# Interleaving two tensors: eight tiles with separate output buffers, or six longer tiles woven in place

## The chip, the cores and the metric

The kernel runs on one core of a Trainium2 chip. The metric is the device time of one execution in microseconds. Three timed runs of the kernel before gave a median of 314.32 us, from 314.16 to 314.33.

A core has five engines that run their own instruction streams, and this kernel uses three of them. VectorE copies data inside the on-chip memory (SBUF, 128 partitions). SyncE (SP) and ScalarE (ACT) only issue transfers here: SP the loads, ACT the stores. The transfers themselves run on 16 DMA engines, which both issuing engines share. SP's transfers form one queue and ACT's another. Engines wait for each other, and for transfers, through semaphores; a transfer adds 16 to its semaphore when all of it has landed.

## The reference

`x` and `y` are float32 of shape 32 x 256 x 1024, 33.55 MB each. The output alternates their elements along the last axis:

```python
result = np.zeros((batch, seq, dim * 2), dtype=np.float32)
result[..., 0::2] = x
result[..., 1::2] = y
```

No arithmetic is done. 67.11 MB have to be read and 67.11 MB written. Since the interleaving runs along the last axis, the three tensors can be treated as flat: output elements 2i and 2i + 1 are x[i] and y[i].

## The kernel before

The flat inputs are cut into n = 8 tiles of 128 x 8192 elements. In a tile each partition holds W = 8192 consecutive elements of x and of y, 32 KiB each, and the 64 KiB of output that belong to them. H = 4096 is half of W.

There are two buffers for x (`xt`), two for y (`yt`) and two for the output (`ot`), each of 32 KiB per partition. Tile k uses `xt[k % 2]` and `yt[k % 2]`. Its output is made in two halves, h = 0 and h = 1, and half h always uses `ot[h]`.

- **Loads (SP, lines 42 to 53).** Tile 0's x comes in two DMAs of 16 KiB rows, every later x and every y in one DMA of 32 KiB rows (4 MiB). The first two tiles' loads are issued without a wait. From tile 2 on, x of tile k waits until VectorE has made the third copy of tile k - 2, and y until the fourth, by the counter `woven`.
- **Copies (VectorE, lines 55 to 70).** For each half: one copy of 4096 columns of x into the even columns of `ot[h]` (L67), one of 4096 columns of y into the odd ones (L70). From tile 1 on, the x copy waits until the store of the half before in the same buffer has landed (`osem[h]`). That makes 32 copies.
- **Stores (ACT, lines 72 to 86).** Each half is stored in one DMA of 32 KiB rows as soon as its two copies are done. The very first is cut in two, 8 KiB and 24 KiB of each row, with a semaphore of its own for the first part.
- **End (lines 88 to 94).** ACT waits for the last store from `ot[0]` and clears semaphores; SP waits for the last store from `ot[1]`.

The order on each engine is the order of the code. There is no planner. One extra step in `tile_interleave_kernel` moves the first two DMAs of SP ahead of the barrier that opens the program, so that they are issued at 0.00 and 0.42 us; the next load is issued at 1.90 us.

Of the kernel before, what the change touches and what calls it, by code (L numbers as in the profile page):

```python
# [3 lines left out]


def _interleave(nc, x, y, out):
    P = 128
    W = 8192
    H = W // 2  # L10

    total = 1
    for s in x.shape:
        total *= s
    n = total // (P * W)
    assert n * P * W == total

    def rows(ap, names, k):
        flat = ap.rearrange("b s d -> (b s d)")
        return flat[k * names : (k + 1) * names].rearrange("(p w) -> p w", p=P)  # L20

    fp32 = mybir.dt.float32
    xt = [nc.alloc_sbuf_tensor(f"xt{b}", [P, W], fp32).ap() for b in (0, 1)]
    yt = [nc.alloc_sbuf_tensor(f"yt{b}", [P, W], fp32).ap() for b in (0, 1)]
    ot = [nc.alloc_sbuf_tensor(f"ot{b}", [P, W], fp32).ap() for b in (0, 1)]

    xsem = [nc.alloc_semaphore(f"xsem{b}") for b in (0, 1)]
    hsem = nc.alloc_semaphore("hsem")
    qsem = nc.alloc_semaphore("qsem")
    ysem = [nc.alloc_semaphore(f"ysem{b}") for b in (0, 1)]  # L30
    woven = nc.alloc_semaphore("woven")
    osem = [nc.alloc_semaphore(f"osem{b}") for b in (0, 1)]


    cuts = [0, W // 4, W]
    parts = [slice(a, b) for a, b in zip(cuts, cuts[1:])]

    xs = [rows(x, P * W, k) for k in range(n)]
    ys = [rows(y, P * W, k) for k in range(n)]
    os_ = [rows(out, 2 * P * W, k) for k in range(n)]  # L40

    nc.sync.dma_start(out=xt[0][:, :H], in_=xs[0][:, :H]).then_inc(xsem[0], 16)
    nc.sync.dma_start(out=xt[0][:, H:], in_=xs[0][:, H:]).then_inc(hsem, 16)

    for k in range(n):
        b = k % 2
        if k >= 2:
            nc.sync.wait_ge(woven, 4 * (k - 2) + 3)
        if k:
            nc.sync.dma_start(out=xt[b], in_=xs[k]).then_inc(xsem[b], 16)  # L50
        if k >= 2:
            nc.sync.wait_ge(woven, 4 * (k - 2) + 4)
        nc.sync.dma_start(out=yt[b], in_=ys[k]).then_inc(ysem[b], 16)

    for k in range(n):
        b = k % 2
        for h in (0, 1):
            c = slice(h * H, (h + 1) * H)
            if h == 0:
                nc.vector.wait_ge(xsem[b], 16 * (k // 2 + 1))  # L60
            elif k == 0:
                nc.vector.wait_ge(hsem, 16)
            if k:
                nc.vector.wait_ge(osem[h], 16 * k)
            if (k, h) == (1, 0):
                nc.vector.wait_ge(qsem, 16)
            nc.vector.tensor_copy(out=ot[h][:, 0::2], in_=xt[b][:, c]).then_inc(woven, 1)  # L67
            if h == 0:
                nc.vector.wait_ge(ysem[b], 16 * (k // 2 + 1))
            nc.vector.tensor_copy(out=ot[h][:, 1::2], in_=yt[b][:, c]).then_inc(woven, 1)  # L70

    for k in range(n):
        for h in (0, 1):
            nc.scalar.wait_ge(woven, 4 * k + 2 * h + 2)
            if (k, h) == (0, 0):
                for c in parts[:-1]:
                    nc.scalar.dma_start(
                        out=os_[k][:, c], in_=ot[h][:, c]
                    ).then_inc(qsem, 16)
                c = parts[-1]  # L80
                nc.scalar.dma_start(out=os_[k][:, c], in_=ot[h][:, c]).then_inc(osem[h], 16)
                continue
            nc.scalar.dma_start(
                out=os_[k][:, h * W : (h + 1) * W], in_=ot[h]
            ).then_inc(osem[h], 16)

    nc.scalar.wait_ge(osem[0], 16 * n)
    used = sorted(s.num for s in [*xsem, hsem, qsem, *ysem, woven, osem[0]])
    assert used == list(range(used[0], used[-1] + 1)), used
    nc.scalar.sem_clear(range(used[0], used[-1] + 1))  # L90
    nc.sync.nop(nofuse=True).wait_op(osem[1], 16 * n, "sem-ge").then_inc(
        osem[1], -16 * n
    )


def kernel(tc, x, y, out):
    nc = tc.nc
    tc.close()
    tc.compile()

    _interleave(nc, x, y, out)

    blocks = nc.main_func.blocks
    for engine in (mybir.EngineType.SP, mybir.EngineType.SP):
        opening = blocks[0].instructions
        at, moved = next(
            (b, i)
            for b in blocks[1:]
            for i in b.instructions
            if i.engine == engine and i.opcode == "DMACopy"  # L110
        )
        assert not (moved.sync_info and moved.sync_info.on_wait)
        body = at.instructions
        body.remove(moved)
        gate = next(
            n
            for n, i in enumerate(opening)
            if i.engine == engine and i.opcode == "Drain"
        )
        opening.insert(gate, moved)  # L120
        at.instructions = body
        blocks[0].instructions = opening


# [1 line left out]
_INS = ['x', 'y']  # L126
_OUTS = [((32, 256, 2048), 'float32')]


# [23 lines left out]
```

## Time and profile before

| What | us |
|---|---|
| median of three runs | 314.32 |
| span of the profiled execution, first to last instruction | 312.9 |
| what lies around the span (median less span) | 1.4 |
| VectorE busy, 32 copies | 72.0 |
| VectorE waiting at L67 for stores to land | 206.5 |
| one copy of 128 x 4096, L67 and L70 | 2.295 and 2.288 |
| a 4 MiB store, issue to landing (median) | 34.1 |
| a 4 MiB load of y, issue to landing (median) | 41.5 |

The profiled execution's own time is its span and what lies around it; its page lists the span alone. A page shows, for 40 equal slices of the span, the busy tenths of an engine and of the 16 DMA engines together. The time from issue to landing of a transfer holds the time that it stood behind others in its queue. q1 in the profile is SP's queue, the loads; q10 is ACT's, the stores.

### The profile page before, as it was taken

The page shows a single profiled execution, that of the slowest core. Times are in us where ns is not written, and L with a number is a line of the kernel's source. Part 1 is how long each engine was busy: PE and PEld are TensorE (multiplying, and loading weights), DVE is VectorE, ACT ScalarE, POOL GpSimd, SP SyncE. Part 2 cuts the span into 40 slices and gives each one's busy share as a digit, 9 for nine tenths or more (in the row PEclk, how much of TensorE's full clock was granted, in tenths as well). Part 3 has the DMA queues.
Part 4 walks back from the last instruction along what each step waited for, and adds up shares of the span by engine and source line. Part 5 has one row for each costly group of instructions (what it writes and reads, how often), then busy time and mean ns, then how long its engine had stood idle before and what let it go on. Part 6 is the DMA issues. An engine that isn't in the chain of part 4 may idle for free.

```text
span 312.9 us, 114 instructions
## 1 busy us (share of the span) xinstructions
DVE 72.0 (23%) x32; POOL 0.2 (0%) x4
## 2 busy tenths in 40 slices
DVE  0216000501305023050220503205032050415410
POOL 0000000000000000000000000000000000000000
DMA  8999999999999999999999999999999999999998
GB/s 337 467 402 436 436 402 419 452 457 415 427 444 411 461 402 469 402 469 402 469 402 465 406 440 432 423 448 402 469 402 469 402 469 402 469 402 448 423 423 381
DMA packets 4896, 134.22 MB, mean 429 GB/s; under 512 B 544, under 2 KB 544, under 8 KB 544
## 3 DMA queue, kind: packets, MB, share of 16 engines
q1 hardware_dynamic: 2448, 67.11, 50.1%
q10 hardware_dynamic: 2448, 67.11, 49.7%
HBM read 67.11 MB, written 67.11 MB: 429 GB/s over the span
## 4 chain that ended last, share of the span: by engine, by line
DMA 82%; DVE 12%; issue 0%
DMA out_dram<-ot 76%; DMA yt<-in_y_dram 6%; DVE ot L70 6%; DVE ot L67 6%
## 5 line engine op out<-in xcount | busy, mean ns | idle before, releaser
L67 DVE COPY ot<-xt 128x4096 f32<-128x4096 f32 x16 | 36.7, 2295 | 213.8 <-DMA out_dram<-ot 206.5
L70 DVE COPY ot<-yt 128x4096 f32<-128x4096 f32 x16 | 36.6, 2288 | 12.3 <-DMA yt<-in_y_dram 12.3
L137 POOL MEMSET const-bfloat16-1.0<- 128x1 bf16 x1 | 0.1, 103 | 0.0
L137 POOL MEMSET const-uint8-127<- 128x1 uint8 x1 | 0.1, 102 | 0.0
L137 POOL MEMSET const-float32-0.0<- 128x1 f32 x1 | 0.1, 100 | 0.2 <-issue 0.2
L137 POOL MEMSET const-float32-1.0<- 128x1 f32 x1 | 0.1, 99 | 0.0
## 6 DMA issues: line engine op xcount, KB each, us to landing
out_dram<-ot ACTq DMA_DIRECT2D x15, 4096.0 KB, 34.1
yt<-in_y_dram SPq DMA_DIRECT2D x8, 4096.0 KB, 41.5
xt<-in_x_dram SPq DMA_DIRECT2D x7, 4096.0 KB, 24.3
xt<-in_x_dram SPq DMA_DIRECT2D x2, 2048.0 KB, 9.5
out_dram<-ot ACTq DMA_DIRECT2D x1, 3072.0 KB, 32.8
out_dram<-ot ACTq DMA_DIRECT2D x1, 1024.0 KB, 16.3
```

The lines of the kernel that those rows point to most:

```text
L67: nc.vector.tensor_copy(out=ot[h][:, 0::2], in_=xt[b][:, c]).then_inc(woven, 1)
L70: nc.vector.tensor_copy(out=ot[h][:, 1::2], in_=yt[b][:, c]).then_inc(woven, 1)
L137: nc = _bacc.Bacc("TRN2", target_bir_lowering=False, num_devices=1)
```

## The change

The tiles become six: five of 11008 columns and one of 10496, so that rows of a load are 43 KiB (41 KiB in the last tile). There are no separate output buffers. Instead there are two regions `R[0]` and `R[1]` of 86 KiB per partition. Tile k of N columns uses `R[k % 2]`: x is loaded into its first N columns, y into the next N, and the 2N output elements are made in the same place. The first half of the region then holds the output of the first N/2 pairs ("low"), the second half that of the others ("high"). Two smaller buffers help: `park` of N/2 columns, and `last` of 2752.

With h = N/2, VectorE makes these copies for a tile, in this order:

1. the upper half of x into `park`;
2. the lower half of x spread to the even columns of low, from the top down: first the columns h/2 to h (they go to columns h to 2h, where the parked half of x was), then the columns 0 to h/2 by way of `last`, since their targets overlap them: three copies;
3. after y has landed, the lower half of y to the odd columns of low. Low is complete, and ACT stores it;
4. the upper half of y to the odd columns of high, the first h/2 directly and the other h/2 by way of `last`: three copies;
5. `park` to the even columns of high. High is complete, and ACT stores it.

That is nine copies per tile, three of h columns and six of h/2: 54 in all. Each copy but the first carries a wait, in the instruction itself, for the copy before it to be complete (`step`). With the separate waits for x (six, and one for the first part of tile 0) and for y (six) the code issues 67 VectorE instructions; the short description of the change counts 81, and the code does not say what the other 14 are.

A load of x of tile k >= 2 waits until low of tile k - 2 has been stored, and a load of y until high of tile k - 2 has been stored. x of tile 0 comes in two DMAs, 16 KiB and 27 KiB of each row; VectorE waits for both. The first store, low of tile 0, is issued in two parts, 8 KiB and 35 KiB of each row, with one semaphore for both. There are 13 loads and 13 stores, where there were 17 and 17.

```diff
@@ -4,92 +4,128 @@
 from concourse import mybir
 
 
+TILES = [11008] * 5 + [10496]
+FIRST = 4096
+EARLY = 2048
+
+
 def _interleave(nc, x, y, out):
     P = 128
-    W = 8192
-    H = W // 2
+    n = len(TILES)
+    N_MAX = max(TILES)
 
     total = 1
     for s in x.shape:
         total *= s
-    n = total // (P * W)
-    assert n * P * W == total
+    assert sum(TILES) * P == total
+    assert all(N % 2 == 0 for N in TILES)
 
-    def rows(ap, names, k):
+    starts = [sum(TILES[:k]) for k in range(n)]
+
+    def rows(ap, words, k):
         flat = ap.rearrange("b s d -> (b s d)")
-        return flat[k * names : (k + 1) * names].rearrange("(p w) -> p w", p=P)
+        a = starts[k] * P * words
+        return flat[a : a + TILES[k] * P * words].rearrange("(p w) -> p w", p=P)
 
     fp32 = mybir.dt.float32
-    xt = [nc.alloc_sbuf_tensor(f"xt{b}", [P, W], fp32).ap() for b in (0, 1)]
-    yt = [nc.alloc_sbuf_tensor(f"yt{b}", [P, W], fp32).ap() for b in (0, 1)]
-    ot = [nc.alloc_sbuf_tensor(f"ot{b}", [P, W], fp32).ap() for b in (0, 1)]
+    R = [nc.alloc_sbuf_tensor(f"R{b}", [P, 2 * N_MAX], fp32).ap() for b in (0, 1)]
+    park = nc.alloc_sbuf_tensor("park", [P, N_MAX // 2], fp32).ap()
+    SPARE = 2752
+    last = nc.alloc_sbuf_tensor("last", [P, SPARE], fp32).ap()
 
     xsem = [nc.alloc_semaphore(f"xsem{b}") for b in (0, 1)]
-    hsem = nc.alloc_semaphore("hsem")
-    qsem = nc.alloc_semaphore("qsem")
+    fsem = nc.alloc_semaphore("fsem")
     ysem = [nc.alloc_semaphore(f"ysem{b}") for b in (0, 1)]
-    woven = nc.alloc_semaphore("woven")
-    osem = [nc.alloc_semaphore(f"osem{b}") for b in (0, 1)]
+    step = nc.alloc_semaphore("step")
+    lsem = [nc.alloc_semaphore(f"lsem{b}") for b in (0, 1)]
+    hsem = [nc.alloc_semaphore(f"hsem{b}") for b in (0, 1)]
+
+    xs = [rows(x, 1, k) for k in range(n)]
+    ys = [rows(y, 1, k) for k in range(n)]
+    os_ = [rows(out, 2, k) for k in range(n)]
 
 
-    cuts = [0, W // 4, W]
-    parts = [slice(a, b) for a, b in zip(cuts, cuts[1:])]
+    count = 0
 
-    xs = [rows(x, P * W, k) for k in range(n)]
-    ys = [rows(y, P * W, k) for k in range(n)]
-    os_ = [rows(out, 2 * P * W, k) for k in range(n)]
+    def copy(to, of):
+        nonlocal count
+        made = nc.vector.tensor_copy(out=to, in_=of)
+        if count:
+            made = made.wait_op(step, count, "sem-ge")
+        made.then_inc(step, 1)
+        count += 1
 
-    nc.sync.dma_start(out=xt[0][:, :H], in_=xs[0][:, :H]).then_inc(xsem[0], 16)
-    nc.sync.dma_start(out=xt[0][:, H:], in_=xs[0][:, H:]).then_inc(hsem, 16)
+    def halvings(m):
+        while m > SPARE:
+            assert m % 2 == 0
+            yield m // 2, m
+            m //= 2
+        yield 0, m
 
-    for k in range(n):
+    done = []
+    for k, N in enumerate(TILES):
+        b = k % 2
+        h = N // 2
+        X = R[b][:, :N]
+        Y = R[b][:, N : 2 * N]
+        low = R[b][:, :N]
+        high = R[b][:, N : 2 * N]
+
+        if k == 0:
+            nc.vector.wait_ge(fsem, 16)
+        nc.vector.wait_ge(xsem[b], 16 * (k // 2 + 1))
+        copy(park[:, :h], X[:, h:])
+        for i, j in halvings(h):
+            if i:
+                copy(low[:, 2 * i : 2 * j : 2], X[:, i:j])
+            else:
+                copy(last[:, :j], X[:, :j])
+                copy(low[:, 0 : 2 * j : 2], last[:, :j])
+        nc.vector.wait_ge(ysem[b], 16 * (k // 2 + 1))
+        copy(low[:, 1::2], Y[:, :h])
+        done.append([count])
+        for i, j in halvings(h):
+            i, j = h - j, h - i
+            if j < h:
+                copy(high[:, 2 * i + 1 : 2 * j : 2], Y[:, h + i : h + j])
+            else:
+                copy(last[:, : j - i], Y[:, h + i : h + j])
+                copy(high[:, 2 * i + 1 : 2 * j : 2], last[:, : j - i])
+        copy(high[:, 0::2], park[:, :h])
+        done[-1].append(count)
+
+    nc.sync.dma_start(out=R[0][:, :FIRST], in_=xs[0][:, :FIRST]).then_inc(fsem, 16)
+    nc.sync.dma_start(
+        out=R[0][:, FIRST : TILES[0]], in_=xs[0][:, FIRST:]
+    ).then_inc(xsem[0], 16)
+    for k, N in enumerate(TILES):
         b = k % 2
         if k >= 2:
-            nc.sync.wait_ge(woven, 4 * (k - 2) + 3)
+            nc.sync.wait_ge(lsem[b], 16 * (k // 2) + (16 if b == 0 else 0))
         if k:
-            nc.sync.dma_start(out=xt[b], in_=xs[k]).then_inc(xsem[b], 16)
+            nc.sync.dma_start(out=R[b][:, :N], in_=xs[k]).then_inc(xsem[b], 16)
         if k >= 2:
-            nc.sync.wait_ge(woven, 4 * (k - 2) + 4)
-        nc.sync.dma_start(out=yt[b], in_=ys[k]).then_inc(ysem[b], 16)
+            nc.sync.wait_ge(hsem[b], 16 * (k // 2))
+        nc.sync.dma_start(out=R[b][:, N : 2 * N], in_=ys[k]).then_inc(ysem[b], 16)
 
-    for k in range(n):
+    for k, N in enumerate(TILES):
         b = k % 2
-        for h in (0, 1):
-            c = slice(h * H, (h + 1) * H)
-            if h == 0:
-                nc.vector.wait_ge(xsem[b], 16 * (k // 2 + 1))
-            elif k == 0:
-                nc.vector.wait_ge(hsem, 16)
-            if k:
-                nc.vector.wait_ge(osem[h], 16 * k)
-            if (k, h) == (1, 0):
-                nc.vector.wait_ge(qsem, 16)
-            nc.vector.tensor_copy(out=ot[h][:, 0::2], in_=xt[b][:, c]).then_inc(woven, 1)
-            if h == 0:
-                nc.vector.wait_ge(ysem[b], 16 * (k // 2 + 1))
-            nc.vector.tensor_copy(out=ot[h][:, 1::2], in_=yt[b][:, c]).then_inc(woven, 1)
+        for c, sem, ready in zip((0, N), (lsem[b], hsem[b]), done[k]):
+            nc.scalar.wait_ge(step, ready)
+            cuts = [c, c + N]
+            if (k, c) == (0, 0):
+                cuts = [0, EARLY, N]
+            for i, j in zip(cuts, cuts[1:]):
+                nc.scalar.dma_start(out=os_[k][:, i:j], in_=R[b][:, i:j]).then_inc(sem, 16)
 
-    for k in range(n):
-        for h in (0, 1):
-            nc.scalar.wait_ge(woven, 4 * k + 2 * h + 2)
-            if (k, h) == (0, 0):
-                for c in parts[:-1]:
-                    nc.scalar.dma_start(
-                        out=os_[k][:, c], in_=ot[h][:, c]
-                    ).then_inc(qsem, 16)
-                c = parts[-1]
-                nc.scalar.dma_start(out=os_[k][:, c], in_=ot[h][:, c]).then_inc(osem[h], 16)
-                continue
-            nc.scalar.dma_start(
-                out=os_[k][:, h * W : (h + 1) * W], in_=ot[h]
-            ).then_inc(osem[h], 16)
-
-    nc.scalar.wait_ge(osem[0], 16 * n)
-    used = sorted(s.num for s in [*xsem, hsem, qsem, *ysem, woven, osem[0]])
+    assert n % 2 == 0
+    nc.scalar.wait_ge(hsem[0], 16 * (n // 2))
+    nc.scalar.wait_ge(lsem[1], 16 * (n // 2))
+    used = sorted(s.num for s in [*xsem, fsem, *ysem, step, *lsem, hsem[0]])
     assert used == list(range(used[0], used[-1] + 1)), used
     nc.scalar.sem_clear(range(used[0], used[-1] + 1))
-    nc.sync.nop(nofuse=True).wait_op(osem[1], 16 * n, "sem-ge").then_inc(
-        osem[1], -16 * n
+    nc.sync.nop(nofuse=True).wait_op(hsem[1], 16 * (n // 2), "sem-ge").then_inc(
+        hsem[1], -16 * (n // 2)
     )
```

## The prediction

> **What bounds the kernel now.** I read the page from the top: which engine is busy, then the DMA rows, then the chain that ended last, then rates by stretch, then DMA issues.
>
> ```profile
> span 312.9 us, 114 instructions
> ...
> DVE 72.0 (23%) x32; POOL 0.2 (0%) x4
> ...
> DMA  8999999999999999999999999999999999999998
> ...
> q1 hardware_dynamic: 2448, 67.11, 50.1%
> q10 hardware_dynamic: 2448, 67.11, 49.7%
> HBM read 67.11 MB, written 67.11 MB: 429 GB/s over the span
> ```
>
> VectorE works 23% of the span. The 16 DMA engines are 9 or more tenths busy in every slice but the first and last, and the load queue (q1) and the store queue (q10) together fill 99.8%. The bytes, 134.22 MB, are fixed by the problem. So the transfers bound the kernel, and an edit counts only if it changes what the DMA engines spend per byte or leaves both queues empty at once. VectorE's 206.5 us of waiting for stores costs nothing in itself. The chain confirms it; columns are start, length, what:
>
> ```profile
> 76.83 2.29 DVE ot L67
> 79.12 2.21 DVE ot L70
> ...
> 81.36 34.17 DMA out_dram<-ot
> 115.53 0.02 issue
> 115.55 2.29 DVE ot L67
> ```
>
> A period is 115.55 - 76.83 = 38.72 us, and it moves four DMAs of 4 MiB (two loads, two stores): 9.68 us each. In the trace's packet records a row is one packet, and rows of 8, 16, 24 and 32 KiB take 309, 611, 912 and 1213 ns: 301.3 ns per 8 KiB and some 8 ns fixed, with 9 ns for the packet that signals completion. Each engine carries 8 rows of a DMA.
>
> Rates by stretch (start:end, length, DVE, POOL, clock, DMA share, GB/s) show where the engines are not at that pace:
>
> ```profile
> 0.00:7.00 7.00, 0.00 (x0) 0.20 (x4) 1.00 0.88 337
> ...
> 27.00:32.00 5.00, 1.61 (x1) 0.00 (x0) 1.00 0.96 375
> ...
> 115.00:270.00 155.00, 35.97 (x16) 0.00 (x0) 1.00 1.01 434
> ```
>
> Against 434 GB/s the start loses 7 x (1 - 337/434) = 1.6 us, and 27 to 32 us, when the first store begins beside the loads, 5 x (1 - 375/434) = 0.7 us. Nothing else is lost before the last slice.
>
> ```profile
> xt<-in_x_dram SPq DMA_DIRECT2D x2, 2048.0 KB, 9.5
> ...
> out_dram<-ot ACTq DMA_DIRECT2D x1, 1024.0 KB, 16.3
> ```
>
> The 1 MiB store is 8 rows of 8 KiB per engine, 2.5 us alone; it took 16.3. Issued at 24.24, its first packet came at 28.64 (4.4 us, 3.6 load rows), and then each small row waited for one 32 KiB load row: 8 x (0.31 + 1.21) = 12.2. So the queues take turns row by row.
>
> **The change, part by part.** Sums are against this execution: 312.9 us of span and 314.32 - 312.9 = 1.4 us to the median around it, which I leave as it is (three runs within 314.16 to 314.33).
>
> *Fewer, longer rows.* Loads go from 17 DMAs to 13, stores from 17 to 13: 34 to 26, and data packets per engine from 272 to 208. Overhead per DMA, low end: 9.68 - 32 x 0.3013 = 0.04 us, from the period. High end: 8 x 0.008 + 0.009 = 0.07, from the packet records. Saving 8 x 0.04 = 0.3 to 8 x 0.07 = 0.6. I take 0.3, since the period is a whole elapsed time and packets may overlap a little. Rows over 32 KiB are not in this trace; that they run as one packet at the same pace is an extrapolation (a rival below).
>
> *VectorE.* The code issues 54 copies: per tile three of 5504 columns and six of 2752 (5248 and 2624 in the last). Today's 4096 columns take 2.29. A 5504 copy in proportion is 3.08; a 2752 copy lies between 1.54 (in proportion) and 2.29 (no smaller than the full one). A tile is 18.5 to 23.0 us. The wait in each copy ends the overlap of 0.08 between neighbours (2.29 long, 2.21 apart) and adds some 0.03 of wake-up (copy ends 24.20, ACT's store begins 24.24): 0.1 each, 1 per tile. That is 117 to 145 us in all against 313, hidden by DMA as long as a queue has work. Behind a waiting copy stand only later copies; the store that waits is ACT's, and through the store SP's next load. Two places can lose the cover.
>
> *The first round.* All 23 MB of the first two tiles' loads are issued without a wait. Half a tile is 11008/8192 x 9.68 = 13.0 us of DMA. y0 lands at 21.91 + 2 x 3.33 = 28.6 (today's landing plus the longer halves); after one 3.08 copy ACT issues at 31.7; the first packet follows 4.4 us (as today) to 5.9 us (3.6 rows of 1.63) later: 37. Loads run meanwhile; x1 has 4 left, y1 13. The 8 KiB part takes turns with 43 KiB rows: 8 x (0.31 + 1.63) = 15.5, to 52.5, and y1 has 4 left. The 35 KiB rest (8 rows of 1.33) shares with that until about 60, then runs alone to 67.3. SP's x2 waits for it: the load queue is empty from 60 to 67.7 plus 4.4 to 5.9, about 73. Behind x2 on SP stands y2, which waits for high0 anyway. The engines are not idle, since high0 (ready 31.7 + 3 x 1.54 + 3.08 + waits = 40) follows at once. Cost of this dry load queue: 0 if sharing is as smooth as later, 0.7 at most if the queue's restart costs what the first store did at 27 to 32. Both slow stretches in the trace are first uses of a queue, which a restart is not, so I take 0. The first store's own 0.7 stays.
>
> *Steady state.* From 73 on the load queue switches half a DMA after the store queue (high0 has 7 of 13 left), so each load is issued some 13 us before its turn, and low_k, ready 3.5 us after y_k lands, also has some 9 to spare. Nothing is added.
>
> *The tail.* At 73 the loads have done four halves (52), the stores 13.0 + 5.8: a lead of 33. Equal turns keep it, less 1.2 for the last tile's shorter load rows: 32 at the loads' end. Low5 and high5 are 2 x 12.4 of that, so high4 has 7.2 left. Low5 needs 0.4 for landing, one copy (2.94), and up to 1 us to its first packet (0.99 at the start): 4.4. Margin 2.8 us. High5 needs another 8 to 10 on VectorE, under 12.4 of low5. So nothing is exposed, but this is the thinnest cover.
>
> *Start and end.* Two x0 loads of 16 and 27 KiB rows go out first, instead of two of 16; y0 is issued at about 1.9 as now, with 13 us of loads ahead of it. The final waits stand on two stores as now. 0.
>
> [...]
>
> **Sum:** 314.32 - 0.3 = 314.0.
>
> **The rivals.**
> 1. *Tail gap (slower).* At the end VectorE weaves the first half of the last tile with no store left, so both queues are empty. It decides once high4 has under 4.4 us left when y5 lands, which is when x2's first packet comes after 76 instead of 73. The most it can cost is 4.4 plus the small effects: 315 to 318.4, middle 316. For it: a margin of 2.8 at the end of a long count, and landing, copy and issue in a row before low5. Against: all rows used are from this trace, and the turns were equal in steady state. 0.17.
> 2. *Rows over 32 KiB cut in two (the change doesn't do what it says).* 23 of the 26 DMAs have such rows, 8 more packets each: 184 x 5 to 8 ns = 0.9 to 1.5, less 0.3: 315.1 or a little under. No row in the trace exceeds 32 KiB. With it I count a dry queue's restart at 0.7 and longer rows slowing the first store. 0.10, of which 0.09 beyond +0.2%.
> 3. *A larger gain.* Overhead at the high end (0.6), and the 0.7 loss at 27 to 32 smaller: 313.0 to 313.7. For: the packet records' fixed 8 ns. Against: the first store starts in the same manner. 0.21.
> 4. *Forecast:* transfers stay saturated, 313.7 to 314.9, likeliest 314.0. 0.52.
>
> **Numbers.** 0.2% (0.63 us) is about what a measurement of this kernel can tell from no change. Faster: rival 3, 0.21. Same: 0.52 + 0.01 = 0.53. Slower: 0.17 + 0.09 = 0.26. The range 313.4 to 316.5 leaves out about 0.08 below (rival 3's low part) and 0.08 above (rival 1's upper part). The forecast's own range is 313.7 to 314.9.
>
> **What would show it.** Right: 3328 data packets and 416 completions (q1 and q10 at 1872 each), both queues near 50%, a period of 52.0 us per tile, VectorE at 117 to 145 us, high4 still storing when the last y lands. Rival 1: a slice below 9 tenths near 285 us and a chain with DVE between the last loads and low5. Rival 2: packets well above 1872 per queue. A rate under 434 GB/s where both queues are full would make the whole sum wrong.

## The result and the profile after

The changed kernel took 315.71 us in the median of five runs (314.70 to 316.88), beside 314.27 for the kernel before: a ratio of 1.0046, interval 1.0028 to 1.0064. Run again beside its variants it took 314.87 (11 runs, 314.62 to 315.91) where the kernel before took 314.20: 1.0023, interval 1.0014 to 1.0031. So it is slower, by 0.7 to 1.4 us. Its single times scatter over 2.2 us in the first group and 1.3 in the second; those of the kernel before beside them lie within 0.2 (five runs) and 0.7 (35 runs). The forecast was 0.3 us faster. The profiled execution is the slowest of the five, 316.88 us, of which 315.6 is span; the second profile is of 314.78 us, span 313.5.

The page of the changed kernel, first execution:

```profile
span 315.6 us, 134 instructions
...
DVE 111.1 (35%) x54; POOL 0.2 (0%) x4
...
DMA  9999999999999999999999999999999999999994
...
q1 hardware_dynamic: 1872, 67.11, 49.7%
q10 hardware_dynamic: 1872, 67.11, 49.2%
q14 instruction: 1, 0.01, 0.0%
```

Much is as forecast: 1872 packets in each queue, so a 43 KiB row is one packet, and VectorE's work runs beside the transfers. At 111 us it is under the 117 to 145 forecast. Two things are new. The DMA engines are only 4 tenths busy in the last slice, where they were 8 before. And there is a third queue, q14, with one packet of instructions, which the page of before does not have.

Rates by stretch (start:end, length, DVE, POOL, clock, DMA share, GB/s), in the same execution:

```profile
0.00:7.00 7.00, 0.00 (x0) 0.20 (x4) 1.00 0.95 363
27.00:32.00 5.00, 3.34 (x2) 0.00 (x0) 1.00 0.98 423
...
62.00:72.00 10.00, 8.62 (x5) 0.00 (x0) 1.00 1.02 441
115.00:270.00 155.00, 55.62 (x27) 0.00 (x0) 1.00 1.00 433
...
312.20:315.60 3.40, 0.00 (x0) 0.00 (x0) 1.00 0.06 25
```

The first store's slow stretch has left 27 to 32 us, since the store comes later. From 62 to 72 us the load queue is empty, and the engines are full of stores, as forecast. But the last 3.4 us move 25 GB/s: a share of 0.06 of 16 engines is one engine. The kernel before at its end, and the last stretch of the changed one by the queue view, whose second line is GB/s in 40 slices:

```profile
311.00:312.20 1.20, 0.00 (x0) 0.00 (x0) 1.00 1.01 437
312.20:312.90 0.70, 0.00 (x0) 0.00 (x0) 1.00 0.01 0
```

```profile
DMA  0088000008000008000000800000000000000000
GB/s 0 0 365 365 0 0 0 0 0 365 0 0 0 0 0 365 0 0 0 0 0 0 365 0 0 0 0 0 0 0 0 0 0 0 0 0 0 0 0 0
```

Views that start at 311 us count a row where it begins. In the changed kernel five rows of 41 KiB begin after 311.0, on three engines; all others are on their last row or done.

The packet records tell which engine is late. With few exceptions a row begins within some 10 ns of the end of the row before it on its engine, so the records can be threaded into 16 chains, each with the same bytes: 8 rows of every DMA. When the chains end, and what lies between the first and the last engine's completion of a DMA (us):

```
                              first    median   last     spread of completions over the run
before                        312.24   312.35   312.48   0.40 for the first loads, then 0.24 to the end
changed, first execution      311.97   312.16   315.20   loads 0.49, 2.66 from the third tile's x on, 4.85 at the end
changed, second execution     312.02   312.20   313.03   loads 0.43, 0.55 from the third tile's x on, 1.01 at the end
```

The median engine is done 0.15 to 0.2 us sooner than before. The kernel waits for the last, which is 3.0 and 0.8 us behind the median where it was 0.1.

### The profile page after: what moved, and what is told of

It reads as the page before. It is cut to its first block, busy times and chain, and to the rows that moved or that the text cites. A ratio compares the mean times of both kernels' runs of the same rounds, so it can differ in the third digit from the quotient of the medians.

```text
span 315.6 us, 134 instructions
## 1 busy us (share of the span) xinstructions
DVE 111.1 (35%) x54; POOL 0.2 (0%) x4
## 3 DMA queue, kind: packets, MB, share of 16 engines
q1 hardware_dynamic: 1872, 67.11, 49.7%
q10 hardware_dynamic: 1872, 67.11, 49.2%
## 4 chain that ended last, share of the span: by engine, by line
DMA 55%; another core or an unknown queue 32%; DVE 5%; SPq 0%; issue 0%; ACTq 0%; DVEq 0%
DMA R<-in_y_dram 31%; DMA out_dram<-R 24%; DVE R L52 5%; DVE last L52 0%; SPq L106 0%; ACTq L119 0%; SPq L109 0%; DVEq L84 0%
## 5 line engine op out<-in xcount | busy, mean ns | idle before, releaser
L52 DVE COPY R<-R 128x2752 f32<-128x2752 f32 (+3 forms) x18 | 37.0, 2058 | 90.9 <-DMA R<-in_y_dram 90.5
L52 DVE COPY park<-R 128x5504 f32<-128x5504 f32 (+1 forms) x6 | 18.0, 3005 | 90.2 <-DMA R<-in_x_dram 90.2
L52 DVE COPY R<-last 128x2752 f32<-128x2752 f32 (+1 forms) x12 | 19.0, 1585 | 0.4
L52 DVE COPY last<-R 128x2752 f32<-128x2752 f32 (+1 forms) x12 | 19.0, 1582 | 0.4
L52 DVE COPY R<-park 128x5504 f32<-128x5504 f32 (+1 forms) x6 | 18.0, 3006 | 0.2
```

Of the source, the lines that this page charges most:

```text
L52: made = nc.vector.tensor_copy(out=to, in_=of)
```

## The experiments

Theory R (restart): when the load queue runs empty and starts again, chance throws a DMA engine or two out of step with the others, and these lose time that is never made up, since each engine has its own rows (8 of every DMA in the packet records). Theory I (instructions): the packet in q14 delays the engine that carries it. Theory L (length): rows of 43 KiB drift apart by themselves. Each group of runs below is beside runs of the kernel before on the same chip, with medians of 314.20 to 314.25.

### Without the empty load queue

```diff
-            nc.sync.wait_ge(lsem[b], 16 * (k // 2) + (16 if b == 0 else 0))
+            nc.sync.wait_ge(lsem[b], 16 * (k // 2))
...
-            if (k, c) == (0, 0):
-                cuts = [0, EARLY, N]
```

> The changed kernel with the first store in one DMA of 43 KiB rows instead of 8 KiB and 35 KiB rows. Theory R (restart): in the changed kernel the load queue runs empty from 62 to 72 us, at its restart one or two of the 16 DMA engines fall out of step, and these lose about 0.6 us at later boundaries of DMAs until they end 2 to 3 us behind the rest. Without the split, the first half lands some 4 us sooner, so the gap in the load queue shrinks to nothing or little: the engines end within 0.5 us of each other and the time is about 314.0 (313.4 to 314.3). Theory L (long rows): 43 KiB rows as such let engines drift; the spread at the end stays 2 to 3 us and the time 315.2 to 316. Theory S (split): the change of row size inside the first store costs all engines 0.65 us at 49.8 us; without it 0.5 less, and nothing else changes: 315.1.

Measured: 315.12 (314.92 to 315.32), ratio 1.0028, interval 1.0018 to 1.0038. The load queue no longer runs empty. The scatter shrinks to 0.4 us, the loss stays, so R alone doesn't carry it. The profile has the packet in q14 at 260.6 us, and the first store now costs every engine 1.1 us at 34 us, where the changed kernel lost 0.6 at 49.8 us, as its first store went over from 8 KiB to 35 KiB rows. So theory S of the expectation does not hold: without the split that loss is not saved but comes earlier and is larger. One engine loses another 1.0 at 34 us: stores then complete over 2.75 us and loads over 1.13, and both stay so for 180 us. Long rows therefore did not drift by themselves here in steady state, which speaks against L in that form.

The same kernel with one wait more:

```diff
+        if k == 2:
+            nc.sync.wait_ge(hsem[0], 16)
```

> As the kernel with the first store in one DMA, but the third tile's x also waits until the second half of the first tile is stored, which leaves the load queue empty for some 15 us (about 71 to 90). The store queue has work all that time. Theory R: the engines fall out of step at the restart and the last engine ends 1 to 3 us behind: 315 to 316.5. Theory L: as without the extra wait. If emptying the queue costs nothing, the same time as without the extra wait, within 0.3.

Measured: 315.55 (315.41 to 315.98, four runs), 0.43 above the run without the wait. That is within R's range, but the profile doesn't show R's mechanism. The load queue is empty from 74.9 to 85.7 us, and the spread of the loads is 0.60 before and after. The edit empties the store queue as well, from 130.1 to 140.9 us, and the spread of the stores is 0.60 before that and 2.06 behind it. The last engine ends at 313.66 against a median of 312.49: 0.83 of these 1.2 us are at 262.5 us, where the packet in q14 comes, and 0.25 at 155.7. So this run does not tell what an emptied load queue costs by itself.

### An emptied load queue in the kernel before

```diff
+        if k == 2:
+            nc.sync.wait_ge(osem[0], 16)
```

> The kernel before, with one more wait: the third tile's x is issued only when the first half tile's store has landed (about 57 us), so the load queue is empty from about 46 to 60 us, with 32 KiB rows and separate output buffers. Theory R: engines out of step, spread of the completions above 1 us where it was 0.25, and 315 to 316.5. Theory L: the spread stays 0.25 and the time 314.3 within 0.2.

Measured: 314.86 (314.19 to 315.22), ratio 1.0019, interval 1.0010 to 1.0028. One execution of ten lost nothing, and the others less than the 315 to 316.5 expected. The profile shows how one of them lost its time. The load queue is empty from 46.5 to 55.6 us. From 0.25 us the spread of the loads' completions jumps to 2.09 at the third tile's x, the first load after the restart. The time lost is 1.0 us on one engine, which ends at 313.24 where the median is 312.27. The end of that execution:

```profile
311.00:312.30 1.30, 0.00 (x0) 0.00 (x0) 1.00 0.82 353
312.30:313.60 1.30, 0.00 (x0) 0.00 (x0) 1.00 0.00 0
```

No row begins in the last 1.3 us; a straggler is ending its last. There are 32 KiB rows, no q14 and the old copies here, so R holds by itself: 0.6 us in the median for one restart, and in one execution nothing.

```diff
-    cuts = [0, W // 4, W]
+    cuts = [0, W]
...
-            if (k, h) == (1, 0):
-                nc.vector.wait_ge(qsem, 16)
```

> The kernel before with its first store in one DMA of 32 KiB rows instead of 8 and 24 KiB. If the loss of 0.7 us at 27 to 32 us belongs to the split, it goes: 313.7. If it belongs to the first use of the store queue, it stays: 314.2, with 0.04 saved for one DMA less.

Measured: 314.39 (314.28 to 314.63), ratio 1.0006, interval 0.9997 to 1.0015. Every engine still loses 0.7 us when stores begin (0.6 before), so in this kernel the loss belongs to the stores' start and not to the split.

### Rows, copies and instructions

```diff
+            for i, j in ((0, N // 2), (N // 2, N)):
+                nc.sync.dma_start(out=R[b][:, i:j], in_=xs[k][:, i:j]).then_inc(xsem[b], 16)
...
-            cuts = [c, c + N]
+            cuts = [c, c + N // 2, c + N]
```

> The changed kernel with each load (from the second tile on, and tile 0's y) and each store after the first issued as two DMAs of half the columns, so that no row but the first store's second part exceeds 27 KiB; tiles, copies and waits stay, and the load queue still runs empty once. 23 more DMAs at 0.04 us add 0.9 us to every engine. If out-of-step engines lose time because rows are long (Theory L+R: a restart throws an engine out of step, and long rows make it lose 0.4 to 0.7 us again and again), the spread at the end falls to about 1 us, as in the kernel before with an emptied load queue, and the time is 314.5 to 315.3. If the length of rows has nothing to do with it, the spread stays 3 us and the time is 316 to 317.

Measured: 316.47 (316.19 to 318.81, four runs). Median engine 315.2, last 317.1 in the profiled one, which is the run of 318.81, so what follows is this one execution. The engines as a whole end 3 us later, of which 0.9 had been allowed, and the spread at the end is still 2 us. But the load queue did not run empty here, as the expectation had assumed: the third tile's x is issued at 63.0 us, while y of the second loads until 75.3. The spread of the loads is 1.08 at 44 us, after the stores have begun, and 3.55 at 62. So stragglers need neither long rows nor an emptied queue. The other 2 us are a gap at the tail. y of the last tile lands on the last engine at 285.7 us, 5.9 behind the first; the copy that completes low5 runs from 286.3 to 289.2, and 14 of the 16 engines begin its store between 290.0 and 290.2, ten of them after 1.5 to 2.2 us without work. From 288 to 290 us the DMA share is 0.28. That is the prediction's rival 1, brought about by a late engine.

```diff
-                copy(last[:, :j], X[:, :j])
-                copy(low[:, 0 : 2 * j : 2], last[:, :j])
+                pass
...
-                copy(last[:, : j - i], Y[:, h + i : h + j])
-                copy(high[:, 2 * i + 1 : 2 * j : 2], last[:, : j - i])
+                pass
```

> The changed kernel without the four copies per tile that go through the spare buffer, so that part of the output is left unwoven: 30 VectorE copies instead of 54. All transfers stay. Theory I (instruction fetch): the one 8 KiB instruction packet inside the span, at 263 us near VectorE's 64th instruction, disappears, and the engine that carried it loses 0.6 to 0.8 us less; the spread at the end becomes smaller where that engine was one of the last, so 0 to 0.8 us faster than the changed kernel. Theory R: the engines that fell out of step at the restart still end 2 to 3 us late, so 315.2 to 316. If VectorE's work were the cause, 314.0.

Measured: 314.77 (314.04 to 316.34, twelve runs), ratio 1.0016, interval 1.0004 to 1.0027. The profiled execution, of 314.09 us:

```profile
span 312.8 us, 110 instructions
...
DMA  9999999999999999998999989999999999999997
...
q1 hardware_dynamic: 1872, 67.11, 50.0%
q10 hardware_dynamic: 1872, 67.11, 49.6%
```

No q14. The load queue runs empty as before, yet here no engine fell out of step: the spread is 0.43 at the third tile's x and 0.42 at the end, the median engine ends at 312.08 and the last at 312.39. All transfers are those of the changed kernel. This is what the forecast had in mind, and this one execution is 0.16 us under the median of the kernel before. The median of the twelve lies under the 315.2 to 316 of theory R, and only 0.10 under the changed kernel's 314.87. The other runs reach to 316.34; that the restart makes the difference among them is argued, and no trace of them shows it.

```diff
+            for i in range(4):
+                at = 4 * (2 * k + h) + i
+                nc.vector.memset(tiny[:, at : at + 1], 0.0)
```

> The kernel before with 64 more VectorE instructions, each setting one column of a scratch tile, behind the copies. Their own time (some 0.06 us each) is hidden. Theory I: an instruction packet appears inside the span, and one DMA engine ends 0.5 to 0.8 us behind: 314.7 to 315.0. Otherwise 314.2 as without.

Measured: 314.86 (314.77 to 315.18), ratio 1.0019, interval 1.0010 to 1.0027. The packet comes at 178.0 us. Its DMA engine is late by 0.302 us at that point and its next row takes 0.533 longer than the usual 1.213; it ends at 313.17 where the median engine ends at 312.27. The 64 instructions themselves take 1.3 us in all, on VectorE, which is idle for three quarters of the time.

```diff
+            cut = N // 2 if k == 1 else N
+            nc.sync.dma_start(out=R[b][:, :cut], in_=xs[k][:, :cut]).then_inc(xsem[b], 16)
+            if k == 1:
+                nc.sync.dma_start(out=R[b][:, cut:N], in_=xs[k][:, cut:]).then_inc(xsem[b], 16)
```

> The changed kernel with its first store in one DMA, and the second tile's x, which is loading when the first store begins, in two DMAs of 22 KiB rows instead of one of 43 KiB. Every engine lost 1.1 us at 34 us where 43 KiB loads met a first store of 43 KiB rows, and 0.55 to 0.65 us where loads were 32 KiB. If the loss goes by the length of the load row in flight, it falls to some 0.5 us and the time from 315.1 to about 314.6. If it goes by the stored row, it stays 1.1 and the time is 315.1.

Measured: 322.84 (321.23 to 324.01, five runs), on top of the kernel with its first store in one DMA at 315.12. At 34 us every engine again loses about 1.0 us, so the loss does not go by the load row. But the kernel with one more DMA is 7.7 us slower:

```profile
55.00:95.00 40.00, 17.63 (x9) 0.00 (x0) 1.00 1.00 402
95.00:280.00 185.00, 64.47 (x32) 0.00 (x0) 1.00 1.00 431
280.00:311.00 31.00, 10.38 (x5) 0.00 (x0) 1.00 0.95 409
311.00:319.90 8.90, 0.00 (x0) 0.00 (x0) 1.00 0.75 326
```

At a DMA share of 1.00, 55 to 95 us run at 402 GB/s: rows take longer. Four things stand in this execution, of 321.23 us. From 59 to 83 us, 49 stored rows take 0.1 to 0.85 us more than 1.63, each right after its engine has loaded the row of the same number of its DMA; half of the engines have them. All other stored rows keep to 1.63, some 70 more after a load of the same number among them, so the same number alone is not enough. At 66 and 91 us most engines lose up to 1.3 in a load; the store queue is empty from 84.6 to 92.1. Loads lose more around 180, 222 and 245 us. And y of the last tile lands only at 288.3, so that 11 engines stand idle for 0.3 to 3.3 us before low5's store at 292.5: rival 1's gap again. The last engine ends at 319.5. Why cutting one load brings all this was not settled.

### Once more, and versions with both causes removed

The changed kernel again, unedited:

> The changed kernel once more, beside its variants on one chip. Theory R: which engines fall out of step when the load queue restarts at 72 us is chance, so single times differ by 1 to 2 us (314.5 to 317) with a median near 315.5, and in the profile a few engines end 1 to 3 us behind the rest, which end near 312.1 of the span as they did. A theory with a fixed cost would give times within 0.3 us of each other.

Measured: 314.87 (314.62 to 315.91). The scatter is there, but narrower than expected: nine of eleven lie within 314.62 to 315.04. In the profile the spread is 0.50 before the restart and 0.55 after it, so no engine fell far out of step. Two engines end late all the same: the one that carried the packet in q14 at 257.1 us, at 313.03, and one that took 0.35 us longer in two loads, at 220.8 and 246.5, at 312.94. In this execution the packet alone, taken away, would have gained 0.1 us.

The next kernel is the changed one with both edits, the first store in one DMA and no copies through the spare buffer:

> The changed kernel with its first store in one DMA and without the copies through the spare buffer (part of the output is left unwoven): neither an empty load queue nor, by theory I, an instruction packet inside the span. Theories R and I together: the engines stay in step apart from what the first store itself does at 34 us (1.1 us on all), so 314.1 to 314.5 with times close together. If an engine is thrown out of step by the first store as well, as in the profile with all copies, 314.8 to 315.2. Theory L (long rows drift by themselves): 315 or more.

Measured: 314.69 (314.41 to 314.97), ratio 1.0012, interval 1.0003 to 1.0020, some 0.2 above the 314.1 to 314.5 expected. No q14; the spread stays 0.86, as it was when the first store began. The median engine ends at 312.58, 0.4 later than in the changed kernel: it loses 1.35 us as the first store begins, against 0.7 to 0.8 with the split. Against the first store in one DMA with all copies (315.12) the missing copies and their packet are worth 0.43.

```diff
+    def park_copy(to, of, sem, value):
...
+        made = nc.gpsimd.tensor_copy(out=to, in_=of)
+        made.wait_op(sem, value, "sem-ge").then_inc(psem, 1)
...
-        copy(park[:, :h], X[:, h:])
+        park_copy(park[:, :h], X[:, h:], xsem[b], 16 * (k // 2 + 1))
...
-        copy(high[:, 0::2], park[:, :h])
+        park_copy(high[:, 0::2], park[:, :h], step, count)
```

> The changed kernel with the two park copies of each tile on GpSimd instead of VectorE, which leaves VectorE 42 copies and fewer waits; the output is complete. Transfers are the same, so by R and I: no instruction packet for VectorE inside the span, 0.3 to 0.8 us faster than the changed kernel on average, still with the lottery of the restart: median 314.5 to 315.2. If the instruction packet comes anyway, 315.3 to 316.

Measured: 314.62 (314.33 to 316.04, twelve runs), ratio 1.0013, interval 1.0005 to 1.0022. There is no q14 with 54 recorded VectorE instructions (72 in the changed kernel). The profiled execution, of 314.60 us, has a span of 313.0: 1.6 us lie around it instead of 1.3, and so in all twelve. So what the missing packet saved inside the span, the kernel with GpSimd's copies gave back by 0.3 outside it.

The same edit on the kernel with its first store in one DMA:

> The same with the first store in one DMA: no empty load queue, no instruction packet, complete output. By R and I the best of the six-tile kernels: 314.1 to 314.5, close to the kernel before, since 0.3 us saved on 8 DMAs stands against 0.5 us more at the first store. 315 or above would speak for a further cost of the long rows.

Measured: 314.95 (314.64 to 315.18), ratio 1.0020, interval 1.0011 to 1.0028. The last engine ends at 312.66 with no q14 and no restart, and again 1.6 us lie around the span. The expectation missed by 0.45 us, and 0.3 of it is the time around the span. The profiled execution is the fastest of the eleven, so what the others lost is not seen. No version tried beats the kernel before.

### How many instructions

Two kernels test theory I by itself: the kernel before with 12 and with 28 one-column settings more on VectorE, and nothing else (57 and 73 recorded VectorE instructions).

```diff
+            if k < 2:
+                for i in range(3):   # 7 in the second kernel
+                    at = 16 * k + 8 * h + i
+                    nc.vector.memset(tiny[:, at : at + 1], 0.0)
```

> The kernel before with 12 one-column settings of a scratch tile more on VectorE, 57 recorded VectorE instructions. Theory I with a limit between 57 and 72: no instruction packet inside the span and 314.2 within 0.15, all engines ending within 0.3 us. If any added instruction costs, 314.4 or more.

> The kernel before with 28 such instructions more, 73 recorded VectorE instructions, one more than the changed kernel has. Theory I: one instruction packet inside the span and one DMA engine 0.8 us behind the rest: 314.7 to 315.0. If the number of instructions is not what brings it, 314.2.

Measured: 314.22 (314.15 to 314.31), ratio 1.0000, interval 0.9990 to 1.0009, and 314.76 (314.73 to 315.03), ratio 1.0018, interval 1.0009 to 1.0026. First the page with 12 more, then with 28 more:

```profile
span 312.9 us, 126 instructions
...
DMA  8999999999999999999999999999999999999999
...
q1 hardware_dynamic: 2448, 67.11, 50.1%
q10 hardware_dynamic: 2448, 67.11, 49.7%
```

```profile
span 313.4 us, 142 instructions
...
DMA  8999999999999999999999999999999999999997
...
q1 hardware_dynamic: 2448, 67.11, 50.0%
q10 hardware_dynamic: 2448, 67.11, 49.6%
q14 instruction: 1, 0.01, 0.0%
```

Sixteen instructions of 59 ns, all executed in the first 82 us, make the kernel 0.54 us slower. In the second kernel the DMA engine with the packet is held up for 0.302 us at 216.6 and 0.533 more in its next row. It ends at 313.03; the median engine ends at 312.30. That the packet belongs to VectorE's code is inferred from when it comes: in all eight profiles that have it VectorE had begun 60 to 66 of its recorded instructions, at 178 us in one kernel and at 269 in another, and the profiles with at most 57 have none.

## Why the prediction was wrong

**What failed.** The sum treated 16 engines as one. Its step on VectorE, "hidden by DMA as long as a queue has work", counted the copies' time and not their number; that time was hidden. The code of 72 recorded instructions, though, comes with a packet of 8 KiB at 257 to 263 us. It falls on a DMA engine whose rows there begin within 4 ns of the end of the row before, so the next row is late: in the first execution, with the packet at 263.30, it begins at 263.605 instead, and takes 2.086 us instead of 1.552. The packet takes 0.309 us, with its aftermath about 0.84 (0.306 and 0.534 there; 0.302 and 0.533, 0.835 in all, in the two versions of the kernel before that have the packet), all on one engine. That is 0.7 beyond the 0.1 us by which the last engine trails anyway, and with 0.15 saved on the median engine it comes to 0.55. The second profiled execution, of 314.78 us, is 0.58 above 314.20, though a second engine was nearly as late there; in the kernel before with 28 instructions more, where no other engine was, it is 0.54. In the changed kernel it shows in the fastest executions: none of 16 is under 314.62, while without the copies by way of the spare buffer, and so without the packet, five of twelve lie at 314.04 to 314.32. The median gained only 0.10, since other engines are late as well. Of the 1.44 us in the first five runs the packet is thus about 0.55; the rest is put down to the second failed step, the queue below. Instructions as DMA traffic were in no step and no rival. The short description of the change counts 81 VectorE instructions where the code issues 67, which was noted and not followed.

**The dry load queue.** The times were right: empty from 62 to 72 where 60 to 73 was forecast, the first half landed at 68.4 for 67.7. "So I take 0" was wrong as a mean and right for some executions: the spread of the loads grew by 0.05 us or nothing there in three profiles (the second of the changed kernel, fewer copies, GpSimd), by 2.1 in the first. The times tell the same: in the four groups of six-tile runs whose load queue empties after the split first store, single times scatter over 1.3 to 2.3 us, in the three with one first store and no empty queue over 0.4 to 0.6; in the kernel before, the one added wait widens it from 0.3 to 1.0. The bound of 0.7 was for a loss on all engines together. In the first profiled execution two engines lost more than that, and the others nothing but the packet; of the two, the second lost its first 0.25 us only at 98.9 us, so for it the restart is not shown as the cause. The last one, at the restart at 74 us, idled 0.37 us and took 0.60 longer for its first load. Later it lost 0.37, 0.67 and 0.59 in single loads at 141.8, 168.1 and 194.9, each right after it had completed a store, 0.30 at 275.6, and 0.05 in each of five stored rows: 3.1 us in all. That a restart alone can put one engine behind is shown in the kernel before (1.0 us). Why an engine out of step loses more at later boundaries stays open; that chance has a part is seen in the scatter.

**Fewer, longer rows.** The forecast was 0.3, the median engine gained 0.15 to 0.2. The row time was right: 1627 ns for 43 KiB, by the line through the shorter rows (5.375 x 301.3 + 8), and from 115 to 270 us the rate was 433 GB/s beside 434. What was missing is the start of the stores, 0.7 to 0.8 us on each engine instead of 0.6, most of it at 49.8 us, where the first store's 35 KiB rows begin.

**The tail.** Rival 1 didn't happen in the changed kernel. The chain's lines before the last copies (start, length, what):

```profile
248.35 34.28 DMA R<-in_y_dram
282.63 0.03 issue
282.66 0.02 DVEq L84
282.68 0.04 issue
282.72 2.91 DVE R L52
285.63 0.02 issue
```

Low5 goes out at 285.65, and the first engine completes high4 at 287.2, some 9.7 us after its last load at 277.4, where 7.2 had been worked out. The margin was real but thinner than those figures, since y5 had landed on the last engine only at 282.3: the late engine delayed the copy, which waits for all 16 and began at 282.72. Where the lateness of the loads reached 5.9 us, in the kernel with half rows, the gap of rival 1 did open. Rivals 2 and 3 did not happen either.

**The range** held both medians by luck: it had been made wide for a gap at the tail and not for what happened.

## What to carry to other kernels

In these kernels the transfers were saturated and each DMA engine carried 8 rows of every DMA. The span went with the slowest engine (it ended at 312.48 us of 312.9 before, at 315.20 of 315.6 in the first execution of the changed kernel, where the median engine was done at 312.16), and a delay on one was not made up. So look at when each engine ends, beside the mean share. Count the instructions of an engine also as traffic: here the step from 57 to 73 on VectorE cost 0.54 us through one packet on one DMA engine. A saving per DMA of 0.04 us, 8 times, is lost to a single such event or to one restart (0.64 us in the median of the kernel before), so a queue that is let run empty needs a better reason than that.

## What was not expected of the hardware

One 8 KiB instruction packet delayed its DMA engine by about 0.84 us, though it took 0.309: the row after it took 0.533 longer where it had 32 KiB (the kernel before with 28 and with 64 instructions more) and 0.534 where it had 41 (the changed kernel). The start of the stores beside running loads cost every engine about 0.6 us in the kernel before, with first rows of 8 KiB, 0.7 with 32 KiB, and 1.1 to 1.35 with 43 KiB in two versions of the changed one. And one load cut in two came with 7.7 us more, in long rows, loads and a gap at the tail, of which the cause stays open.
